# Four columns abreast in the head, pieces of 512, 384 and 128 features in the tail of a two-block network kernel

## The chip, the cores and the metric

The kernel runs on one core of a Trainium2 chip. Its metric is the device time of one execution in microseconds (us). A core has five engines that run side by side, each with its own order of instructions: TensorE (PE) multiplies matrices, VectorE (DVE) and ScalarE (ACT) work on elements, GpSimd (POOL) and SyncE (SP) do little here; SP issues most of the DMA transfers between the chip's memory (HBM) and the core's on-chip memory (SBUF). TensorE writes to PSUM, eight banks of 512 fp32 columns. Engines wait for each other by semaphores.

## The reference

256 tokens of 1024 features pass through two blocks. The first is a convolution branch and a latent attention branch, gated and added, with a convolutional feed-forward behind them; the second adds 16 meta tokens and runs stick-breaking attention, an MLP, a gated linear recurrence and another MLP. What the change touches is the very start and the very end:

```python
h = rms_norm(x, norm1_g[l])
proj = h @ w_in[l]
a_in, q_c, kv_c, k_rope_in, gates = split_cols(proj, IN_SPLITS)
val, gate = a[..., :CONV_WIDTH], a[..., CONV_WIDTH:]    # a is a_in
u = val * jax.nn.sigmoid(gate)
...
h = h + sq_relu_mlp(hn, mlp_w_up[i], mlp_w_down[i])
h = rms_norm_2(h, norm_final)
return h[:, N_META:]
```

`rms_norm` divides a token's features by the root of their mean square plus 1e-6 and multiplies by a gain.

## The kernel before

**Products.** Everything is fp32, and each product is made from three: a matrix w is split into `wh` (rounded to TensorE's short fp32 form) and `wl = w - wh`, the input x likewise into `Ah` and `Al` (`hh` and `hl` in an MLP), and wh·xh + wl·xh + wh·xl is summed in PSUM. All 128x128 weight blocks lie in HBM in the order of their use, 16 of them in a unit of 1 MB. The class `Stream` brings a unit into a buffer `raw` (three buffers), and splits each half unit (8 blocks): ScalarE casts `wh<-raw` (L229), VectorE subtracts `wl<-raw,wh` (L230). `split()` does the next half unit, `ahead()` runs it up to four halves before TensorE's position, `take()` hands out a block. TensorE runs through the blocks without gaps for nearly the whole kernel; the orders of TensorE and SP, and in the first section of all engines, are those of the code.

**Head.** x comes in four pieces of two 128-row chunks each (x has eight chunks k), between the four quarters of unit 0, all on SP's queue (L469, L222); unit 1 follows in two halves, then the vectors, unit 2 in one transfer, positions and constants. `first_part` (L238, L239) splits a quarter of unit 0, `x_split` makes `Ah` and `Al` of one chunk of x with the norm's gain. The norm's divisor is left out of the products: they are linear in x, and it is multiplied in behind them. For it ScalarE squares x (`sq`), VectorE adds the squares up to `sq0` (a tile named `acc` in the profile), and TensorE multiplies a matrix of ones with it, so that each column has its token's sum in all rows (`ps_tr<-acc,ones`); `rsqrt_row` makes `rstd` of that.

The first products are the convolution's four gates (columns 10 to 13) and four values (6 to 9). `linears` computes several output columns abreast: for each k one product for each column. `linear` computes one column over all k. Before, column 10 and 6 (channel 0) ran abreast, 16 blocks and so all of unit 0; then 11 and 7 one after the other (unit 1), then the ones-times-squares matmul, then columns 12, 8, 13, 9. `gate` multiplies by `rstd` and applies tanh, `glu` forms the gated value `upad`, and puts 31 convolution steps per channel on a list `bg`, from which `linear` takes `n_bg` at a time (`NB`).

**Tail.** The last matrix, `down1`, is used the other way round: `hh` and `hl` are the stationary side (128 tokens), the weights are moved through, so the output has tokens on partitions and 1024 features along the free axis. The tokens come in two halves a = 0, 1; `pieces` cuts the features of each half into PSUM tiles. The 32 inputs k run one after the other over all pieces (`down_product`, three matmuls each), but the last six (`TAIL`) are kept and run piece by piece, so that `finish` and `store` of a piece run beside the matmuls of the next. `finish(a, i)` adds the residual (VectorE, `xt<-ps_mm,r2t,xt`), squares with a sum per token (ScalarE, `sqt`, sum into column i of `sums`), and multiplies by the gain (`gx`). `store(a)` adds the columns of `sums`, takes the root (ScalarE, `rs`), the reciprocal (VectorE), scales the pieces (piece 1 on ScalarE, the others on VectorE) and stores them (piece 1 from ScalarE's queue, the others from SP's).

Of the kernel before, what the change touches and what calls it, by code (L numbers as in the profile page):

```python
# [36 lines left out]
NB = (3, 3, 2, 1, 5, 14)  # L37
# [78 lines left out]
# outputs that are summed side by side, one input chunk after the other  # L116
# [4 lines left out]
}  # L121


def weight_plan():
    plan = []

    def cols(name, c0, nk):
        for k in range(nk):
            plan.append((name, k, c0))

    def cols_abreast(name, c0s, nk):
        for k in range(nk):
            for c0 in c0s:
                plan.append((name, k, c0))

    def groups(name, nk):
        for ms in GROUPS[name]:
            for k in range(nk):
                for m in ms:
                    plan.append((name, k, m * P))  # L140

    cols_abreast("w_a", [10 * P, 6 * P], 8)
    for c in range(1, 4):
        cols("w_a", (6 + 4 + c) * P, 8)
        cols("w_a", (6 + c) * P, 8)
    for m in range(6):
        cols("w_a", m * P, 8)
    for m in range(8):
        cols("w_uq", m * P, 3)
    for m in range(4):  # L150
        cols("w_ukv", m * P, 2)
    for k in range(2):
        for m in range(4):
            plan.append(("w_ukv", k, 512 + m * P))
    for m in range(16):
        cols("w_g" if m in NAT_GATES else "w_a", (14 + m) * P, 8)
# [37 lines left out]
class Stream:  # L194
    """Weights in the order of their use: DMA, then the exact two-part split."""

    def __init__(self, nc, w_ap, raw_pool, split_pool):
        self.nc, self.w = nc, w_ap
        self.raw_pool, self.split_pool = raw_pool, split_pool
        self.raw, self.half, self.done = {}, {}, {}  # L200
        self.n_dma = self.n_half = self.pos = 0
        self.nhalf = (NBLK + HB - 1) // HB

    def dma(self):
        u = self.n_dma
        if u >= NU:
            return
        t = self.raw_pool.tile([P, UB * P], F32, tag="raw", name=f"raw{u}")
        n = min(UB, NBLK - u * UB) * P
        step = n // 2 if u == 1 else n  # L210
        for o in range(0, n, step):
            self.nc.sync.dma_start(out=t[:, o:o + step], in_=self.w[u][:, o:o + step])
        self.raw[u] = t
        self.done[u] = 0
        self.n_dma += 1

    def dma_first(self):
        t = self.raw[0] = self.raw_pool.tile([P, UB * P], F32, tag="raw", name="raw0")
        self.done[0] = 0
        self.n_dma = 1  # L220
        for o in range(0, UB * P, 512):
            self.nc.sync.dma_start(out=t[:, o:o + 512], in_=self.w[0][:, o:o + 512])  # L222
            yield
# [9 lines left out]
    def first_part(self, raw, i):  # L233
        """A quarter of the first unit, whose halves split() has only named."""
        hi, lo = self.half[i // 2]
        r = slice(i % 2 * 512, i % 2 * 512 + 512)
        src = raw[:, i * 512:(i + 1) * 512]
        self.nc.scalar.copy(out=hi[:, r], in_=src)  # L238
        self.nc.vector.tensor_tensor(out=lo[:, r], in0=src, in1=hi[:, r].bitcast(F32), op=ALU.subtract)  # L239
# [4 lines left out]
    def split(self):  # L244
# [10 lines left out]
        if self.native(h):  # L255
            self.half[h] = (src, None)
        else:
            hi = self.split_pool.tile([P, HB * P], F32R, tag="wh", name=f"wh{h}")
            lo = self.split_pool.tile([P, HB * P], F32R, tag="wl", name=f"wl{h}")
            self.half[h] = (hi, lo)  # L260
            if h > 1:
                self.parts(h, src, n, 512 if h < 4 else n)
            self.done[u] += 1
# [37 lines left out]
def build(tc, wall, x_t, meta_t, pos, vec, cst, gw, g_fin, out):  # L301
    nc = tc.nc
    ctx = ExitStack()
    with ctx:
# [14 lines left out]
        def mm_tile():  # L319
            return psum("mm", 3)  # L320
# [140 lines left out]
        # ------------------------------------------------------------ block 1  # L461
# [3 lines left out]
        with tc.manual_schedule(), tc.tile_pool(name="pro", bufs=1) as pro:  # L465
            nc.scalar.dma_start(out=vec_t[:, 0:8], in_=vec[:, 0:8])
            first = w.dma_first()
            for k, _ in zip(range(0, KD, 2), first):
                nc.sync.dma_start(out=xres[:, k:k + 2, R:], in_=x_t[:, k:k + 2, :])  # L469
            w.dma()  # L470
# [11 lines left out]
            tables("natural_log_exp_and_others")  # L482
# [5 lines left out]
            w.split()  # L488
            raw0 = w.raw[0]
            w.split()  # L490
            for i in range(4):
                w.first_part(raw0, i)
                x_split(2 * i)
                x_split(2 * i + 1)
# [36 lines left out]
        # rope factors  # L531
# [45 lines left out]
        for ch in range(4):  # L577
            pg, pv = mm_tile(), mm_tile()
            if ch == 0:
                linears("w_a", [10 * P, 6 * P], xa, 8, [pg[:, :S], pv[:, :S]])  # L580
            else:
                linear("w_a", (10 + ch) * P, xa, 8, pg[:, :S], n_bg=NB[0])
            tg = t272("ta", 3)

            def gate(tg=tg, pg=pg):
                paced(tt(tg[:, :S], pg[:, :S], rstd[:, :S]))
                act(out=tg[:, :S], in_=tg[:, :S], func=AF.Tanh, scale=0.5)

            if ch == 0:
                held = (tg, pv, gate)  # L590
                continue
            if ch > 1:
                gate()
            linear("w_a", (6 + ch) * P, xa, 8, pv[:, :S], n_bg=NB[0])
            if ch == 1:
# [4 lines left out]
                held[2]()  # L600
                glu(0, held[0], held[1])
                gate()
# [31 lines left out]
        # the norm of x * rstd: rstd / sqrt(mean(x^2) * rstd^2 + eps)  # L634
# [26 lines left out]
        # rotated key, shared by the heads  # L661
# [54 lines left out]
        def pv_mla(hp):  # L716
            """Two heads, side by side in the array."""
# [104 lines left out]
        # convolutional feed-forward  # L822
# [32 lines left out]
        # the first block's final norm and the second block's first one in one row  # L855
# [4 lines left out]
        # eps for the tokens that have no first norm  # L860
# [24 lines left out]
        def first_rows():  # L885
            # real tokens: r1 / sqrt(mean((x f)^2) r1^2 + eps) = 1 / sqrt(mean((x f)^2) + eps / r1^2)
# [12 lines left out]
        # ------------------------------------------------------------ stick-breaking attention  # L899
# [164 lines left out]
        # softplus(-lam) = max(-lam, 0) + 2 atanh(e / (2 + e)), e = exp(-|lam|)  # L1064
# [14 lines left out]
        # half of the log of a at r = 1  # L1079
# [24 lines left out]
        # ------------------------------------------------------------ RG-LRU  # L1104
# [30 lines left out]
        def gates(m):  # L1135
# [9 lines left out]
            # t = tanh(log(a) / 2): 1 - a^2 = -t (1 + a)^2  # L1145
# [60 lines left out]
        # the last projection, with the tokens on partitions  # L1206
# [23 lines left out]
        # the pieces of the features, for the two halves of the tokens  # L1230
        pieces = (((0, 512), (512, 512)), ((0, 512), (512, 256), (768, 256)))
# [10 lines left out]

        sums = tmp.tile([P, 2, 4], F32, tag="sums", name="sums", bufs=1)
# [11 lines left out]

        def store(a):
            s = tmp.tile([P, 1], F32, tag="nmx", name="total", bufs=2)
            nc.vector.tensor_reduce(out=s, in_=sums[:, a, :len(pieces[a])], axis=AX.X, op=ALU.add)
            act(out=rs[:, a:a + 1], in_=s, func=AF.Sqrt, scale=1.0 / D, bias=eps_t)
# [93 lines left out]
```

## Time and profile before

| | |
|---|---|
| times of three runs | 974.29, 974.38, 975.68 us; median 974.38 |
| span of the profiled execution | 972.0 us, 17931 instructions; its own device time is not given apart |
| TensorE's stage of the last projection | 873 to 965 us |
| last matmul starts | 964.76 us |
| first product matmul starts | 7.02 us |

The page has one execution. PE is TensorE's matmuls, PEld its weight loads, which run beside them; a "q" behind an engine's name is its queue of DMA issues. In a timeline a row has the start and the duration in us, the engine, the line of the kernel, the operation, out<-in, partitions x elements, and in brackets how long the engine stood idle before and which instruction released it. A matmul row's duration reaches over the start of the next, since matmuls are pipelined; what one costs in a dense stretch is the distance of the starts. An LDWEIGHTS row is the load of a matmul's stationary 128x128 matrix.

### The profile page before, as it was taken

Reading aid. Unit: us, or ns where it says so; the run is one execution under the profiler, and the core shown is the slowest. Engines: PE = TensorE matmul, PEld = TensorE weight load, DVE = VectorE, ACT = ScalarE, POOL = GpSimd, SP = SyncE. Lnnn points to the kernel's source line nnn. Section 1 sums busy time; section 2 is a strip of 40 time slices with the busy share of each in tenths; the row PEclk is TensorE's granted clock in tenths of the full one; section 3 lists DMA queues with packets and bytes.
Section 4 is the critical chain, followed back from the end, with each engine's and each line's share of the span. In section 5 each row is a group of like instructions: output and inputs, shape, how many; then the busy total and the mean of one; then the engine's idle time right before and its main releaser. Section 6 shows DMA issues by size and latency. Waiting matters only on the chain.

```text
span 972.0 us, 17931 instructions
## 1 busy us (share of the span) xinstructions
PE 962.1 (99%) x7350; PEld 923.9 (95%) x7350; DVE 688.5 (71%) x1215; ACT 597.3 (61%) x1037; POOL 6.7 (1%) x38
## 2 busy tenths in 40 slices
PE   9999999999999999999999999999999999999997
PEld 8988889999999999999999999999999999998886
DVE  6999888799999566876686555455587985554443
ACT  7855586777667546555556666444479687774332
POOL 0000000000000000000000000000000000000000
PEclk9999999999999999999999999999999999999999
DMA  8523365545554555333234554544452565555531
GB/s 310 196 86 131 130 223 187 199 172 181 197 190 174 180 182 203 107 111 130 88 131 174 174 177 174 180 173 174 174 208 88 210 222 197 175 178 177 201 117 43
DMA packets 26113, 163.39 MB, mean 168 GB/s; under 512 B 3888, under 2 KB 5424, under 8 KB 6960
## 3 DMA queue, kind: packets, MB, share of 16 engines
q1 hardware_dynamic: 25312, 160.29, 47.1%
q0 software_dynamic: 288, 1.57, 0.4%
q8 instruction: 57, 0.93, 0.4%
q10 hardware_dynamic: 432, 0.40, 0.1%
q14 instruction: 24, 0.20, 0.0%
HBM read 161.20 MB, written 1.05 MB: 167 GB/s over the span
## 4 chain that ended last, share of the span: by engine, by line
PE 95%; DVE 2%; ACT 1%; DMA 1%; issue 0%; SPq 0%; DVEq 0%; ACTq 0%
PE ps_mm L385 88%; PE ps_z L385 4%; PE ps_o L385 1%; PE ps_tr L385 1%; DVE wl L230 1%; DMA xres<-x_t 1%; DVE iu L1172 0%; ACT L346 0%; PE ps_tr L710 0%; DVE gt L379 0%; DVE iu L379 0%; DVE th L382 0%; PE ps_tr L973 0%; ACT th L350 0%; PE ps_tr L1227 0%
## 5 line engine op out<-in xcount | busy, mean ns | idle before, releaser
L230 DVE TENSOR_TENSOR wl<-raw,wh 128x1024 fp32r<-128x1024 f32 (+1 forms) x288 | 349.4, 1217 | 210.1 <-ACT wh L229 208.6
L229 ACT CAST wh<-raw 128x1024 fp32r<-128x1024 f32 (+1 forms) x288 | 298.5, 1042 | 222.1 <-PE ps_mm L385 217.7
L385 PE MATMUL ps_mm<-Ah,wh 128*128 128x256 f32 (+1 forms) x1360 | 390.2, 287 | 1.1 <-ACT Ah L350 1.1
L385 PE MATMUL ps_mm<-Ah,wl 128*128 128x256 f32 (+1 forms) x1360 | 386.5, 284 | 0.2 <-DVE wl L230 0.2
L385 PE MATMUL ps_mm<-Al,wh 128*128 128x256 f32 (+1 forms) x1360 | 385.3, 283 | 0.0
L385 PEld LDWEIGHTS ps_mm<-Ah,wh 128*128 128x128 f32 x1360 | 255.3, 188 | 2.1 <-ACT Ah L350 1.2
L385 PEld LDWEIGHTS ps_mm<-Al,wh 128*128 128x128 f32 x1360 | 256.6, 189 | 0.5 <-DVE Al L370 0.4
L385 PEld LDWEIGHTS ps_mm<-Ah,wl 128*128 128x128 f32 x1360 | 255.8, 188 | 1.0 <-DVE wl L230 0.6
L385 PE MATMUL ps_mm<-hl,wh 128*128 128x272 f32 (+1 forms) x432 | 123.5, 286 | 0.0
L385 PE MATMUL ps_mm<-hh,wh 128*128 128x272 f32 (+1 forms) x432 | 123.4, 286 | 0.0
L385 PE MATMUL ps_mm<-hh,wl 128*128 128x272 f32 (+1 forms) x432 | 123.3, 285 | 0.0
L385 PEld LDWEIGHTS ps_mm<-hh,wl 128*128 128x128 f32 x432 | 81.3, 188 | 0.0
L385 PEld LDWEIGHTS ps_mm<-hh,wh 128*128 128x128 f32 x432 | 81.3, 188 | 0.0
L385 PEld LDWEIGHTS ps_mm<-hl,wh 128*128 128x128 f32 x432 | 81.3, 188 | 0.0
L567 DVE SCALAR_TENSOR_TENSOR cacc<-upad,whalf,cacc 128x256 f32<-128x256 f32 x120 | 57.7, 482 | 1.6
L385 PE MATMUL ps_mm<-wh,hh 128*128 128x512 f32 (+1 forms) x160 | 56.0, 350 | 0.0
L385 PE MATMUL ps_mm<-wh,hl 128*128 128x512 f32 (+1 forms) x160 | 55.9, 349 | 0.0
L385 PE MATMUL ps_mm<-wl,hh 128*128 128x512 f32 (+1 forms) x160 | 55.8, 349 | 0.0
L350 ACT ACTIVATE ta<-ps_mm 128x272 f32<-128x272 f32 (+1 forms) x64 | 25.1, 392 | 49.1 <-PE ps_mm L385 49.0
L385 PE MATMUL ps_mm<-bl,wh 128*128 128x256 f32 (+1 forms) x160 | 45.7, 286 | 0.6 <-DVE bl L362 0.6
L385 PE MATMUL ps_mm<-bh,wh 128*128 128x256 f32 (+1 forms) x160 | 46.0, 288 | 0.0
L385 PE MATMUL ps_mm<-bh,wl 128*128 128x256 f32 (+1 forms) x160 | 45.5, 284 | 0.0
(246 smaller groups left out, 1230.9 us busy)
## 6 DMA issues: line engine op xcount, KB each, us to landing
raw<-wall SPq DMA_DIRECT2D x148, 1024.0 KB, 4.9
raw<-wall SPq DMA_DIRECT2D x3, 512.0 KB, 7.6
raw<-wall SPq DMA_DIRECT2D x4, 256.0 KB, 5.8
xres<-x_t SPq DMA_DIRECT2D x4, 256.0 KB, 6.0
gw_t<-gw POOLq DMA_DIRECT2D x1, 1024.0 KB, 7.9
g_t<-g_fin POOLq DMA_DIRECT2D x1, 512.0 KB, 3.4
out_t<-gx SPq DMA_DIRECT2D x2, 256.0 KB, 2.2
cst_t<-cst SPq DMA_DIRECT2D x1, 337.5 KB, 9.0
```

Of the source, the lines that this page charges most:

```text
L229: self.nc.scalar.copy(out=hi[:, r], in_=src[:, r])
L230: self.nc.vector.tensor_tensor(out=lo[:, r], in0=src[:, r], in1=hi[:, r].bitcast(F32), op=ALU.subtract)
L350: i = nc.scalar.activation(out=out, in_=in_, func=func, **kw)
L385: nc.tensor.matmul(out=out_, lhsT=lhsT, rhs=rhs, start=start, stop=stop, skip_group_check=True)
L567: paced(nc.vector.scalar_tensor_tensor(out=cacc[:, ch, :], in0=upad[:, ch, j:j + S], scalar=wj, in1=cacc[:, ch, :], op0=ALU.mult, op1=ALU. ...
```

## The change

At the head, four columns abreast (10, 6, 11, 7, two channels) for each k take the place of two abreast and two in a row, so units 0 and 1 are used together with x, a quarter unit (four blocks) for each chunk k. x comes in eight pieces of one chunk: four on ScalarE's queue (with the load of ScalarE's function tables moved behind them), four on SP's between the quarters of unit 1, which now comes in four transfers like unit 0. Unit 2, one transfer of 1 MB as before, is the one that is cast in 512-column steps between the squares. The ones-times-squares matmul stands after the gate column of channel 2 (120 product matmuls ahead of it, not 96), and the gates of channels 0 and 1 behind it. `NB[1]` is 4.

At the tail, token half 1 is cut into 512, 384 and 128 features. `finish` forms a running `part` (sum of squares / 1024 plus eps, or plus the part before) on VectorE for all pieces but the last, and `store` takes the root of the last piece's sum with `part` as its bias, without the reduction `total`.

```diff
-NB = (3, 3, 2, 1, 5, 14)
+NB = (3, 4, 2, 1, 5, 14)
...
+FIRST = [10 * P, 6 * P, 11 * P, 7 * P]
...
-    cols_abreast("w_a", [10 * P, 6 * P], 8)
-    for c in range(1, 4):
+    cols_abreast("w_a", FIRST, 8)
+    for c in range(2, 4):
...
             nc.scalar.dma_start(out=vec_t[:, 0:8], in_=vec[:, 0:8])
-            first = w.dma_first()
-            for k, _ in zip(range(0, KD, 2), first):
-                nc.sync.dma_start(out=xres[:, k:k + 2, R:], in_=x_t[:, k:k + 2, :])
-            w.dma()
+            for k in range(4):
+                nc.scalar.dma_start(out=xres[:, k, R:], in_=x_t[:, k, :])
+            tables("natural_log_exp_and_others")
+            for _ in w.dma_parts():
+                pass
+            second = w.dma_parts()
+            for k, _ in zip(range(4, KD), second):
+                nc.sync.dma_start(out=xres[:, k, R:], in_=x_t[:, k, :])
+            next(second, None)
...
-            for i in range(4):
-                w.first_part(raw0, i)
-                x_split(2 * i)
-                x_split(2 * i + 1)
+            for _ in range(4):
+                w.split()
+            for i in range(KD):
+                w.first_part(i)
+                x_split(i)
...
+        heads = [mm_tile() for _ in FIRST]
+        linears("w_a", FIRST, xa, 8, [p_[:, :S] for p_ in heads])
+        for ch in range(2, 4):
             pg, pv = mm_tile(), mm_tile()
...
-            if ch == 1:
+            linear("w_a", (10 + ch) * P, xa, 8, pg[:, :S], n_bg=NB[0])
+            if ch == 2:
                 t = psum("tr", 2)
                 mm(t[:, :S], ones, sq0, True, True)
                 rsqrt_row(t[:, :S], rstd[:, :S], D)
                 tables("exp_and_others")
-                held[2]()
-                glu(0, held[0], held[1])
-                gate()
+                for c_ in range(2):
+                    glu(c_, gate(heads[2 * c_]), heads[2 * c_ + 1])
+            tg = gate(pg)
+            linear("w_a", (6 + ch) * P, xa, 8, pv[:, :S], n_bg=NB[0])
...
-        pieces = (((0, 512), (512, 512)), ((0, 512), (512, 256), (768, 256)))
+        pieces = (((0, 512), (512, 512)), ((0, 512), (512, 384), (896, 128)))
...
+            if i < len(pieces[a]) - 1:
+                s = tmp.tile([P, 1], F32, tag="sm%d" % (i % 2), name="part", bufs=2)
+                stt(s, sums[:, a, i:i + 1], 1.0 / D, part.get(a, eps_t), ALU.mult, ALU.add)
+                part[a] = s
...
-            s = tmp.tile([P, 1], F32, tag="nmx", name="total", bufs=2)
-            nc.vector.tensor_reduce(out=s, in_=sums[:, a, :len(pieces[a])], axis=AX.X, op=ALU.add)
-            act(out=rs[:, a:a + 1], in_=s, func=AF.Sqrt, scale=1.0 / D, bias=eps_t)
+            act(out=rs[:, a:a + 1], in_=sums[:, a, n - 1:n], func=AF.Sqrt, scale=1.0 / D, bias=part[a])
```

ScalarE in the head, behind the last quarter of unit 0. Before: the quarter's cast and the last two chunks of x, then unit 1 (`raw_105`) in steps of 512 columns with the squares between, then unit 2 (`raw_109`). "Waits DMAHW..." is a wait for a transfer.

```order
L238 CAST wh_137<-raw_96 128x512 [waits DMAHW7_49]
L350 ACTIVATE Ah<-xres,vec_t 128x256 [waits DMAHW0_49]
L350 ACTIVATE Ah<-xres,vec_t 128x256
L229 CAST wh_165<-raw_105 128x512 [waits DMAHW1_49]
L229 CAST wh_165<-raw_105 128x512
L350 ACTIVATE sq_131<-xres 128x512
L350 ACTIVATE sq_132<-xres 128x512
L229 CAST wh_174<-raw_105 128x512 [waits DMAHW2_49]
L229 CAST wh_174<-raw_105 128x512
L350 ACTIVATE sq_133<-xres 128x512
L350 ACTIVATE sq_134<-xres 128x512
```

Of the change, from the last quarter of unit 1 (`raw_106`) on; `raw_116` is unit 2.

```order
L243 CAST wh_149<-raw_106 128x512 [waits DMAHW7_49]
L357 ACTIVATE Ah<-xres,vec_t 128x256 [waits DMAHW0_49]
L357 ACTIVATE nones_r<-ones 128x128 [waits DVE_49]
L357 ACTIVATE l_6262<-vec_t 128x8 [waits DMAHW1_49]
L234 CAST wh_185<-raw_116 128x512 [waits DMAHW2_49]
L234 CAST wh_185<-raw_116 128x512
L357 ACTIVATE sq_137<-xres 128x512
L357 ACTIVATE sq_138<-xres 128x512
L234 CAST wh_194<-raw_116 128x512 x2
L357 ACTIVATE sq_139<-xres 128x512
L357 ACTIVATE sq_140<-xres 128x512
```

The squares stood behind the first half of unit 1, and stand now behind the first half of unit 2, whose arrival all four wait for in ScalarE's order.

TensorE in the last projection, one input k: the last three of its five tiles before, the pieces of token half 1 (`ps_mm_10638` is its first piece, 10639 and 10640 the others).

```order
L385 MATMUL ps_mm_10638<-wh293_11059,hh_9451 128x512
L385 MATMUL ps_mm_10638<-wl293_11060,hh_9451 128x512
L385 MATMUL ps_mm_10638<-wh293_11059,hl_9452 128x512
L385 MATMUL ps_mm_10639<-wh293_11059,hh_9451 128x256
L385 MATMUL ps_mm_10639<-wl293_11060,hh_9451 128x256
L385 MATMUL ps_mm_10639<-wh293_11059,hl_9452 128x256
L385 MATMUL ps_mm_10640<-wh293_11059,hh_9451 128x256
L385 MATMUL ps_mm_10640<-wl293_11060,hh_9451 128x256
L385 MATMUL ps_mm_10640<-wh293_11059,hl_9452 128x256
```

The same of the change.

```order
L392 MATMUL ps_mm_10648<-wh293_11069,hh_9461 128x512
L392 MATMUL ps_mm_10648<-wl293_11070,hh_9461 128x512
L392 MATMUL ps_mm_10648<-wh293_11069,hl_9462 128x512
L392 MATMUL ps_mm_10649<-wh293_11069,hh_9461 128x384
L392 MATMUL ps_mm_10649<-wl293_11070,hh_9461 128x384
L392 MATMUL ps_mm_10649<-wh293_11069,hl_9462 128x384
L392 MATMUL ps_mm_10650<-wh293_11069,hh_9461 128x128
L392 MATMUL ps_mm_10650<-wl293_11070,hh_9461 128x128
L392 MATMUL ps_mm_10650<-wh293_11069,hl_9462 128x128
```

The matmuls stay in number and order; three of them per k are wider by 128 columns and three narrower.

VectorE at the very end, from the second piece of token half 1 on, before.

```order
L382 SCALAR_TENSOR_TENSOR xt<-ps_mm,r2t,xt 128x256 [waits PE_49]
L379 TENSOR_TENSOR gx<-xt,g_t 128x256 [waits DVE_49]
L382 SCALAR_TENSOR_TENSOR xt<-ps_mm,r2t,xt 128x256 [waits PE_49]
L379 TENSOR_TENSOR gx<-xt,g_t 128x256 [waits DVE_49]
L1258 TENSOR_REDUCE total<-sums 128x1 [waits Activation_49]
L1260 RECIPROCAL rs_10642<-rs_10642 128x1 [waits Activation_49]
```

And of the change, from the same piece's place on.

```order
L389 SCALAR_TENSOR_TENSOR part<-sums,eps_t 128x1 [waits Activation_49]
L389 SCALAR_TENSOR_TENSOR xt<-ps_mm,r2t,xt 128x384 [waits PE_49]
L386 TENSOR_TENSOR gx<-xt,g_t 128x384 [waits DVE_49]
L389 SCALAR_TENSOR_TENSOR part<-sums,part 128x1 [waits Activation_49]
L389 SCALAR_TENSOR_TENSOR xt<-ps_mm,r2t,xt 128x128 [waits PE_49]
L386 TENSOR_TENSOR gx<-xt,g_t 128x128 [waits DVE_49]
L1268 RECIPROCAL rs_10652<-rs_10652 128x1 [waits Activation_49]
```

The reduction behind the last piece is gone; a sum of one column stands ahead of the second and of the third piece, and waits for ScalarE's squares of the piece before.

More of the change, by code (lines that the diff above doesn't have):

```diff
@@ L200, in __init__ @@
         self.raw, self.half, self.done = {}, {}, {}
+        self.first = {}
         self.n_dma = self.n_half = self.pos = 0
@@ L209, in dma @@
         n = min(UB, NBLK - u * UB) * P
-        step = n // 2 if u == 1 else n
-        for o in range(0, n, step):
-            self.nc.sync.dma_start(out=t[:, o:o + step], in_=self.w[u][:, o:o + step])
+        self.nc.sync.dma_start(out=t[:, :n], in_=self.w[u][:, :n])
         self.raw[u] = t
@@ L215, in dma, with dma_parts @@
         self.n_dma += 1
[L217 to L220, printed above, removed]
+    def dma_parts(self):
+        u = self.n_dma
+        t = self.raw[u] = self.raw_pool.tile([P, UB * P], F32, tag="raw", name=f"raw{u}")
+        self.done[u] = 0
+        self.n_dma += 1
         for o in range(0, UB * P, 512):
-            self.nc.sync.dma_start(out=t[:, o:o + 512], in_=self.w[0][:, o:o + 512])
+            self.nc.sync.dma_start(out=t[:, o:o + 512], in_=self.w[u][:, o:o + 512])
             yield
@@ L231, in parts, with first_part @@
                                          op=ALU.subtract)
-    def first_part(self, raw, i):
+    def first_part(self, i):
         hi, lo = self.half[i // 2]
         r = slice(i % 2 * 512, i % 2 * 512 + 512)
-        src = raw[:, i * 512:(i + 1) * 512]
+        src = self.first[i // 4][:, i % 4 * 512:(i % 4 + 1) * 512]
         self.nc.scalar.copy(out=hi[:, r], in_=src)
@@ L260, in split @@
             self.half[h] = (hi, lo)
-            if h > 1:
-                self.parts(h, src, n, 512 if h < 4 else n)
+            if h > 3:
+                self.parts(h, src, n, 512 if h < 6 else n)
+            else:
+                self.first[u] = self.raw[u]
             self.done[u] += 1
@@ L481, in build @@
                 mm(warm[:, :P], ones, ones, True, True)
-            tables("natural_log_exp_and_others")
             sq = [pro.tile([P, 2, S], F32, tag="sq%d" % k, name="sq%d" % k) for k in range(4)]
@@ L486, in x_split @@
                 split_g(xres[:, k, R:], v("norm1_g", k), ah[:, k, :S], al[:, k, :S])
-            w.split()
-            raw0 = w.raw[0]
-            w.split()
-            for i in range(4):
-                w.first_part(raw0, i)
-                x_split(2 * i)
-                x_split(2 * i + 1)
+            for _ in range(4):
[3 more added lines that the diff above has]
+                x_split(i)
             w.split()
@@ L575, in glu, with gate @@
                 bg.append(lambda ch=ch, j=j: conv_tap(ch, j))
-        for ch in range(4):
-            pg, pv = mm_tile(), mm_tile()
[L579 to L592, printed above, removed]
-                gate()
-            linear("w_a", (6 + ch) * P, xa, 8, pv[:, :S], n_bg=NB[0])
-            if ch == 1:
+        def gate(pg):
+            tg = t272("ta", 3)
+            paced(tt(tg[:, :S], pg[:, :S], rstd[:, :S]))
+            act(out=tg[:, :S], in_=tg[:, :S], func=AF.Tanh, scale=0.5)
+            return tg
+        heads = [mm_tile() for _ in FIRST]
+        linears("w_a", FIRST, xa, 8, [p_[:, :S] for p_ in heads])
+        for ch in range(2, 4):
+            pg, pv = mm_tile(), mm_tile()
+            linear("w_a", (10 + ch) * P, xa, 8, pg[:, :S], n_bg=NB[0])
+            if ch == 2:
                 t = psum("tr", 2)
@@ L599, in build @@
                 tables("exp_and_others")
-                held[2]()
-                glu(0, held[0], held[1])
-                gate()
+                for c_ in range(2):
+                    glu(c_, gate(heads[2 * c_]), heads[2 * c_ + 1])
+            tg = gate(pg)
+            linear("w_a", (6 + ch) * P, xa, 8, pv[:, :S], n_bg=NB[0])
             glu(ch, tg, pv)
@@ L1241, in down_product @@
             mm(o, hl[:, k, ra], wh[:, rc], False, k == NH2 - 1)
+        part = {}
         sums = tmp.tile([P, 2, 4], F32, tag="sums", name="sums", bufs=1)
@@ L1254, in finish @@
             tt(gx[:, a, c0:c0 + n], xm, g_t[:, c0:c0 + n])
+            if i < len(pieces[a]) - 1:
+                s = tmp.tile([P, 1], F32, tag="sm%d" % (i % 2), name="part", bufs=2)
+                stt(s, sums[:, a, i:i + 1], 1.0 / D, part.get(a, eps_t), ALU.mult, ALU.add)
+                part[a] = s
         def store(a):
-            s = tmp.tile([P, 1], F32, tag="nmx", name="total", bufs=2)
-            nc.vector.tensor_reduce(out=s, in_=sums[:, a, :len(pieces[a])], axis=AX.X, op=ALU.add)
-            act(out=rs[:, a:a + 1], in_=s, func=AF.Sqrt, scale=1.0 / D, bias=eps_t)
+            n = len(pieces[a])
+            act(out=rs[:, a:a + 1], in_=sums[:, a, n - 1:n], func=AF.Sqrt, scale=1.0 / D, bias=part[a])
             nc.vector.reciprocal(out=rs[:, a:a + 1], in_=rs[:, a:a + 1])
```

## The prediction

> **What bounds the kernel now.** I read the page from the top: the span, the engines' shares, then the chain that ended last.
>
> ```profile
> span 972.0 us, 17931 instructions
> PE 962.1 (99%) x7350; PEld 923.9 (95%) x7350; DVE 688.5 (71%) x1215; ACT 597.3 (61%) x1037; POOL 6.7 (1%) x38
> ...
> PEclk9999999999999999999999999999999999999999
> ...
> PE 95%; DVE 2%; ACT 1%; DMA 1%; issue 0%; SPq 0%; DVEq 0%; ACTq 0%
> ```
>
> TensorE works for 99% of the span at a full clock, and 95% of the chain is its matmuls. So a change pays only if it shortens TensorE's own stream, or the two ends where TensorE does not run: the start-up and the 7 us behind the last matmul. There are 7350 weight loads (PEld) for 7350 matmuls: every matmul brings its own load. The next view, busy time by stage, has us, then busy us and instructions of PE, PEld, DVE, ACT and POOL, granted clock, DMA share, GB/s.
>
> ```profile
> 7.00:14.00 7.00, 6.95 (x49) 6.19 (x49) 6.00 (x13) 6.05 (x13) 0.00 (x0) 1.00 1.04 399
> 14.00:20.00 6.00, 6.00 (x50) 5.89 (x50) 5.63 (x12) 5.49 (x10) 1.13 (x1) 1.00 1.02 406
> ...
> 41.00:130.00 89.00, 89.00 (x535) 78.38 (x534) 82.41 (x194) 52.25 (x119) 0.00 (x0) 1.00 0.38 131
> ...
> 900.00:950.00 50.00, 50.00 (x269) 42.80 (x268) 21.58 (x19) 18.89 (x18) 0.00 (x0) 1.00 0.42 149
> 950.00:972.00 22.00, 15.03 (x83) 12.82 (x81) 8.59 (x18) 5.03 (x14) 0.00 (x0) 0.90 0.13 48
> ```
>
> Two things matter here. In the last projection (900 to 950 us) TensorE has no gap at all while VectorE and ScalarE stand idle more than half the time: what a matmul costs there is time of the kernel, one for one. In the head (7 to 20 us) the DMA engines are full at about 400 GB/s, so data that is needed early comes no sooner than the bytes ahead of it allow.
>
> **The tail's matmuls (the largest term).** For each of 32 inputs k, token half 1 had nine products 512, 256, 256 columns wide (three each), and gets 512, 384, 128. The number of matmuls and of columns stays. This is TensorE's timeline in that stage; a start minus the one before is what a matmul costs, since neighbours overlap.
>
> ```profile
> 944.54 0.28 PE L385 MATMUL ps_mm<-wh,hh 128*128 128x256 f32 x1
> ...
> 945.25 0.40 PE L385 MATMUL ps_mm<-wh,hh 128*128 128x512 f32 x1
> ...
> 947.35 0.28 PE L385 MATMUL ps_mm<-wh,hh 128*128 128x256 f32 x1
> ```
>
> Six 256-wide ones take 945.25 - 944.54 = 0.71 us, 0.118 each; nine 512-wide ones 947.35 - 945.25 = 2.10, 0.233 each. A straight line between them gives 0.176 for 384 columns and 0.061 for 128, and with these 3 x (0.176 + 0.061) = 0.71: no change. But that line holds only while the columns are what takes the time. The trace has narrower matmuls, and they don't follow it (PE and PEld, each in its timeline; x4 and x16 are rows run together):
>
> ```profile
> 790.19 0.50 PE L385 MATMUL ps_tr<-ones,acc 128*128 128x1 f32 x4
> 790.55 0.36 PE L385 MATMUL ps_mm<-Ah,wh 128*128 128x256 f32 x1
> ...
> 790.07 0.54 PEld L385 LDWEIGHTS ps_tr<-ones,acc 128*128 128x128 f32 x4
> 790.52 0.19 PEld L385 LDWEIGHTS ps_mm<-Ah,wh 128*128 128x128 f32 x1
> ...
> 873.28 1.77 PEld L1227 LDWEIGHTS ps_tr<-cst_t,xres 128*128 128x128 f32 x16
> 875.02 0.19 PEld L385 LDWEIGHTS ps_mm<-wh,hh 128*128 128x128 f32 x1
> ...
> 395.03 0.46 PE L385 MATMUL ps_z<-sh,ntri_r 128*128 128x432 f32 x1
> 395.33 0.23 PE L385 MATMUL ps_z<-sh,nones_r 128*128 128x144 f32 x1
> 395.40 0.41 PE L385 MATMUL ps_z<-sl,ntri_r 128*128 128x432 f32 x1
> 395.64 0.23 PE L385 MATMUL ps_z<-sl,nones_r 128*128 128x144 f32 x1
> ```
>
> Four matmuls that move one single column have weight loads that start (790.52 - 790.07) / 4 = 0.1125 us apart, and sixteen 128x128 transposes (875.02 - 873.28) / 16 = 0.109. One column or 128, it is the same: a full 128x128 load takes about 0.11 us, and the next can be prepared only while one matmul runs. Against this speaks a start only 0.07 us after a 144-wide matmul (395.33 to 395.40); but the 432-wide one that follows takes 0.24 us to the next start (395.40 to 395.64), where the line gives 0.20, so the pair costs 0.31, which is 0.20 for the columns and 0.11 for a load, not 0.27. The load is paid there too.
>
> So I take 0.1115 us (between 0.109 and 0.1125, nearest to the transposes and to the single columns alike) for a 128-wide matmul, and 0.176 for a 384-wide one, whose load hides. A k costs 3 x (0.176 + 0.1115) - 0.71 = +0.152 us, and 32 of them **+4.85 us**. Bounds: with 0.109 it is 96 x (0.109 - 0.061) = +4.6; if a narrow load in this type cost as much as a whole 256-wide matmul, 0.118, it would be +5.5; if loads can be prepared further ahead, so that the 384-wide ones' slack covers them (6 x 0.111 = 0.67 is below 0.71), it is 0. The last is a rival below.
>
> The Trainium skill, page "TensorE: Matmul & The Clock Gate", section "Back-to-back issue gap", gives about 81 ns per matmul for a sustained stream of loads and 128-column matmuls, and about 56 ns for an isolated one; by the first this term would be 96 x (0.081 - 0.061) = +1.9 us, by the second nothing. The rows above, 0.109 and 0.1125, speak against both.
>
> **The tail's end.** Behind the last matmul:
>
> ```profile
> 964.76 0.28 PE L385 MATMUL ps_mm<-wh,hl 128*128 128x256 f32 x1
> ...
> 965.07 0.48 DVE L382 SCALAR_TENSOR_TENSOR xt<-ps_mm,r2t,xt 128x256 f32<-128x256 f32 x1 [1.19 <-PE ps_mm L385]
> ...
> 966.19 0.16 DVE L1258 TENSOR_REDUCE total<-sums 128x1 f32<-128x3 f32 x1 [0.18 <-ACT sqt L350]
> ...
> 965.65 0.42 ACT L350 ACTIVATE sqt<-xt 128x256 f32<-128x256 f32 x1 [1.68 <-DVE xt L382]
> 965.98 0.19 ACT L350 ACTIVATION_READ_ACCUMULATOR sqt<-xt 128x1 f32 x1
> 966.38 0.29 ACT L350 ACTIVATE rs<-total,eps_t 128x1 f32<-128x1 f32 x1 [0.22 <-DVE total L1258]
> ...
> L382 DVE SCALAR_TENSOR_TENSOR xt<-ps_mm,r2t,xt 128x512 f32<-128x512 f32 x3 | 2.3, 752 | 6.0 <-PE ps_mm L385 6.0
> L350 ACT ACTIVATE sqt<-xt 128x512 f32<-128x512 f32 x3 | 1.9, 637 | 9.4 <-DVE xt L382 9.4
> ```
>
> The chain is last matmul, residual on VectorE, square on ScalarE, sum, root, reciprocal, scale, store; 972.0 - 964.76 = 7.24 us. At 128 columns the residual is shorter by half the step from 256 to 512, (0.752 - 0.48) / 2 = 0.14; the square likewise by (0.637 - 0.42) / 2 = 0.11; the matmul's own end by some 0.05 (a 144-wide one lasts 0.23, not 0.28). The sum of the three parts goes, with its hand-over: 966.38 - 966.19 = 0.19, of which the direct wait of the root on the square's sums keeps a little; I take -0.17. Together **-0.45** (between -0.2, if only the reduction goes, and -0.7, if the hand-overs halve). The added 128x1 sums stand on VectorE between a piece and the next and wait for ScalarE; behind them waits the next residual, which waits for TensorE anyway (1.19 us in the row above). The 384 piece has 18 x 0.1115 = 2.0 us of the last piece's matmuls for its residual, square and sum, by the rows about 0.62 + 0.53 (half way between 256 and 512 again) + 0.19 (the sums read out) + 0.16 plus hand-overs, some 1.7: covered, by 0.3 us; uncovered, a sum would cost its 0.16. The 384-wide scaling on ScalarE takes about 0.1 longer than the 256 one, beside the 512-wide on VectorE, whose store is issued last.
>
> **The head.** Four columns abreast ask for x half as fast, so TensorE's small stalls there should go.
>
> ```profile
> 6.46 0.91 ACT L350 ACTIVATE Ah<-xres,vec_t 128x256 fp32r<-128x256 f32 x2 [1.48 <-DMA xres<-x_t]
> 12.68 1.15 ACT L229 CAST wh<-raw 128x512 fp32r<-128x512 f32 x2 [0.37 <-DMA raw<-wall]
> 17.10 2.01 ACT L229 CAST wh<-raw 128x1024 fp32r<-128x1024 f32 x2
> ...
> 18.24 0.43 DVE L379 TENSOR_TENSOR acc<-sq 128x256 f32<-128x256 f32 x1
> ...
> 7.02 0.39 PE L385 MATMUL ps_mm<-Ah,wh 128*128 128x256 f32 x1 [1.05 <-ACT Ah L350]
> ...
> 19.76 0.59 PE L385 MATMUL ps_tr<-acc,ones 128*128 128x256 f32 x2
> ...
> 26.32 0.39 PE L385 MATMUL ps_mm<-Ah,wl 128*128 128x256 f32 x1 [0.16 <-DVE wl L230]
> ...
> raw<-wall SPq DMA_DIRECT2D x1, 1024.0 KB, 9.1
> ```
>
> From 7.02 to 26.32 stand 145 product matmuls (145 x 0.118 = 17.1) and the ones-times-squares pair (19.76; 0.47 in steps), so 1.7 us are stalls: that is all the head can gain while the first matmul waits for x at 6.46. What takes their place is the squares. They stood between the casts of unit 1, whose first half came at 12.68, and `acc` was ready at 18.24 + 0.43 = 18.67, 6.0 us later. Now all of unit 1 is cast with x, and the squares stand behind and between the casts of unit 2, which is one transfer of 1 MB. It was issued 9.1 us before it landed, just ahead of the casts at 17.10. The bytes ahead of it are the same (x and units 0 and 1 at 1 MB each, 0.2 MB of vectors), over full DMA engines, so it lands at about 17.2 again. The same four half-unit casts and squares follow: `acc` at 17.2 + 6.0 = 23.2. TensorE, without stalls, has done its 120 products at 7.02 + 120 x 0.118 = 21.2 and waits **2.0 us** there, with every later product behind it. Then 0.47 and 25 products: 23.2 + 0.47 + 25 x 0.118 = 26.6 for the matmul that was at 26.32, **+0.3**. Bounds: unit 2 earlier by 2 us or more, -1.7; later by 1 us, +1.3.
>
> Downstream, the root row and the two gated products come some 5 us later, and the 62 convolution steps behind them. From 41 to 130 us VectorE was busy 82.4 of 89 us: 6.6 us of room, just enough. If not, lost time there is below 1 us; I put none. The fourth background step per chunk (3 to 4) only spreads them.
>
> **Sum.** 972.0 + 4.85 - 0.45 + 0.3 = 976.7 for the span. The median of the runs shown is 974.38, 2.4 above the profiled span; the page gives no device time for the profiled execution, so I take those 2.4 us to lie around the span: **979.1 us**.
>
> **Rivals.**
> 1. *Loads run ahead* (the other side). If several loads can be prepared while a 384 or 512 runs, the 128s stream at 0.061, the first term is 0 and the time 974.3, not slower; it decides from the point where a 128-wide spacing falls below 0.075. For it: the one start 0.07 apart. Against it: the pair's 0.31, and sixteen transposes that never got below 0.109. If the head gains too, 972.3. Chance 0.08, a third of it faster.
> 2. *81 ns a matmul*, loads partly hidden: 979.1 - 4.85 + 1.9 = 976.1. Chance 0.05. This is the rate of the Trainium skill's section named above.
> 3. *The head gains*: unit 2, or x, lands early enough that TensorE finds `acc` ready: 979.1 - 0.3 - 1.7 = 977.1. For it: the first halves and x come in smaller pieces over two queues; against: the DMA engines were already full. Chance 0.15.
> 4. *The head loses*: more transfers with a fixed number in flight, so unit 2 is issued and lands 1.5 us late, and the wait at the squares grows: 980.6. Chance 0.13.
>
> My forecast has 0.59. The range 976.6 to 981.2 takes in rivals 3 and 4 and the bounds of the first term, and leaves out rivals 1 and 2 and the far ends. A measurement of this kernel tells about 0.2% (1.95 us) from no change: slower than 976.33 is 0.86, within 0.09, faster 0.05.
>
> **What would show it.** In the last projection 128-wide matmuls start 0.11 us apart (0.06: rival 1; 0.08: rival 2), and a k takes 2.96 us instead of 2.81. Behind the last matmul 6.8 us instead of 7.24, with the root straight behind the square. The ones-times-squares matmul waits about 2 us for `acc`, near 23 us; no wait there is rival 3. The first matmul near 7.0. The forecast is wrong at once if the last projection is not some 4.9 us longer.

## The result: 0.69% slower, by two terms that add up

The changed kernel takes 980.89 us (median of 4 runs, 980.65 to 981.87) against 974.34 us before; the ratio is 1.0069, 95% interval 1.0056 to 1.0082. The profiled execution spans 979.1 us, 7.0 more than before (979.05 and 972.04 by the traces; the page rounds). The chain and the stages of the changed kernel's page, in the columns used before:

```profile
span 979.1 us, 17945 instructions
...
PE 88%; DVE 7%; DMA 2%; ACT 1%; issue 1%; SPq 0%; ACTq 0%; DVEq 0%
...
7.00:14.00 7.00, 6.12 (x49) 5.91 (x50) 5.90 (x12) 6.11 (x13) 0.00 (x0) 1.00 0.88 283
...
900.00:950.00 50.00, 50.00 (x255) 43.12 (x254) 20.83 (x17) 17.48 (x18) 0.00 (x0) 1.00 0.45 158
```

In the last projection TensorE is still busy in all of the 50 us, but gets through 255 matmuls, not 269. Its share of the chain fell by 7 points, from 95% to 88%; VectorE got five of them, the transfers and the issuing one each. For the first 66 us the chain now runs almost wholly through transfers, the casts and squares on ScalarE and VectorE's splits and convolution steps. TensorE's timeline at four places, the head, the convolution's norm, the start and the end of the last projection:

```profile
7.87 0.39 PE L392 MATMUL ps_mm<-Ah,wh 128*128 128x256 f32 x1 [1.35 <-ACT Ah L357]
...
24.14 0.70 PE L392 MATMUL ps_tr<-acc,ones 128*128 128x256 f32 x2 [1.53 <-DVE acc L386]
...
138.00 1.35 PE L392 MATMUL ps_tr<-upad,ones 128*128 128x256 f32 x5 [0.79 <-ACT upad L357]
...
878.21 0.47 PE L392 MATMUL ps_mm<-wh,hh 128*128 128x512 f32 x1
...
972.53 0.27 PE L392 MATMUL ps_mm<-wh,hl 128*128 128x128 f32 x1
```

Setting matmul n of one kernel beside matmul n of the other (both have 7350) gives how late the changed kernel is:

| place | before, us | after, us | late by |
|---|---|---|---|
| first product matmul | 7.02 | 7.87 | 0.85 |
| 146th product matmul (end of the head) | 26.32 | 27.63 | 1.31 |
| first block products of the attention branch's queries | 63.78 | 65.67 | 1.88 |
| ones times `upad` (convolution's norm) | 135.07 | 138.00 | 2.94 |
| first matmul of the last projection | 875.05 | 878.21 | 3.16 |
| last matmul | 964.76 | 972.53 | 7.77 |
| end | 972.04 | 979.05 | 7.01 |

So 3.2 us are lost ahead of the last projection, nearly all of it in the first 140 us, 4.6 in the last projection, and 0.76 are won behind the last matmul. Single profiles scatter: in the six that have the code of before up to the last projection, it starts between 874.96 and 876.04 us, so a few tenths ahead of it mean nothing. Inside the last projection the kernels that share its code agree to 0.01 us.

### The profile page after: what moved, and what is told of

Its sections match the earlier page's. It is cut to its first block, busy times and chain, and to the rows that moved or that the text cites. A ratio compares the mean times of both kernels' runs of the same rounds, so it can differ in the third digit from the quotient of the medians.

```text
span 979.1 us, 17945 instructions
## 1 busy us (share of the span) xinstructions
PE 967.2 (99%) x7350; PEld 928.5 (95%) x7350; DVE 689.1 (70%) x1218; ACT 596.1 (61%) x1039; POOL 6.7 (1%) x38
## 4 chain that ended last, share of the span: by engine, by line
PE 88%; DVE 7%; DMA 2%; ACT 1%; issue 1%; SPq 0%; ACTq 0%; DVEq 0%
PE ps_mm L392 82%; PE ps_z L392 4%; DVE wl L235 2%; DVE cacc L576 2%; DMA raw<-wall 1%; PE ps_o L392 1%; DMA xres<-x_t 1%; PE ps_tr L392 1%; DVE iu L1175 0%; DVE gt L386 0%; DVE iu L386 0%; DVE th L389 0%; PE ps_tr L976 0%; ACT L353 0%; ACT th L357 0%
## 5 line engine op out<-in xcount | busy, mean ns | idle before, releaser
L392 PE MATMUL ps_mm<-wh,hh 128*128 128x512 f32 (+2 forms) x160 | 57.9, 362 | 0.0
L392 PE MATMUL ps_mm<-wh,hl 128*128 128x512 f32 (+2 forms) x160 | 57.4, 358 | 0.0
L392 PE MATMUL ps_mm<-wl,hh 128*128 128x512 f32 (+2 forms) x160 | 57.2, 357 | 0.0
```

What stands on the lines that cost most here:

```text
L392: nc.tensor.matmul(out=out_, lhsT=lhsT, rhs=rhs, start=start, stop=stop, skip_group_check=True)
```

## The experiments

Eleven kernels ran; each time stands beside runs of the kernel before on the same chip.

### The tail

**Part and bias alone.** The kernel before with `part` and the root's bias, pieces still 512, 256, 256.

```diff
+                stt(s, sums[:, a, i:i + 1], 1.0 / D, part.get(a, eps_t), ALU.mult, ALU.add)
...
-            nc.vector.tensor_reduce(out=s, in_=sums[:, a, :len(pieces[a])], axis=AX.X, op=ALU.add)
-            act(out=rs[:, a:a + 1], in_=s, func=AF.Sqrt, scale=1.0 / D, bias=eps_t)
+            act(out=rs[:, a:a + 1], in_=sums[:, a, n - 1:n], func=AF.Sqrt, scale=1.0 / D, bias=part[a])
```

> The kernel before with the running part and the root's bias alone, pieces 512, 256, 256. My theory, that the sum behind the last square is what this edit removes: the way from the last matmul to the end falls from 7.24 to about 7.0 us, all else stays, about 974.1 us (-0.2). Rival, that the added sums hold VectorE up ahead of the last piece: no gain, or 974.5. Theory and rival lie within the noise of the time; the distance from the last matmul to the end tells them apart.

Measured: 973.55 us, ratio 0.9992 (0.9983 to 1.0001). From the last matmul to the end it is 7.08 us by the trace instead of 7.29, and 7.10 in the kernel with `NB[1]` at 4 below, which has the same tail: the 0.2 of the theory. But "all else stays" was wrong. From the first to the last matmul of the last projection it takes 88.82 us (874.96 to 963.78), where the kernel before has 89.71; the two other kernels below with part, bias and pieces of 256 have 88.82 too, and the head alone, with the old tail, 89.71. The 512-wide matmuls start closer there, nine of them in 2.04 us, before in 2.09 (the kernel before, then this one):

```profile
951.55 0.40 PE L385 MATMUL ps_mm<-wh,hh 128*128 128x512 f32 x1
...
953.64 0.39 PE L385 MATMUL ps_mm<-wh,hh 128*128 128x512 f32 x1
```

```profile
951.43 0.39 PE L385 MATMUL ps_mm<-wh,hh 128*128 128x512 f32 x1
...
953.47 0.39 PE L385 MATMUL ps_mm<-wh,hh 128*128 128x512 f32 x1
```

Why an edit of VectorE's and ScalarE's work does that is not shown.

**The whole tail on the old head.**

```diff
-        pieces = (((0, 512), (512, 512)), ((0, 512), (512, 256), (768, 256)))
+        pieces = (((0, 512), (512, 512)), ((0, 512), (512, 384), (896, 128)))
```

(with part and bias as above)

> The head of before with the whole tail of the change (pieces 512, 384, 128, part and bias). Theory, that a 128-wide matmul costs a weight load, 0.11 us: +4.8 in the last projection, -0.65 behind the last matmul, together +4.1, 978.4 us. Rival, that the growth between 875 us and the last matmul comes from the later start of the stream (another phase of the transfers, or splits that fall behind): at most +0.5, 974.8 or less.

Measured: 978.76 us, ratio 1.0045 (1.0031 to 1.0059), +4.6 beside 974.13. The stretch of one input k in its timeline:

```profile
940.34 0.34 PE L385 MATMUL ps_mm<-wh,hh 128*128 128x384 f32 x1
940.52 0.34 PE L385 MATMUL ps_mm<-wl,hh 128*128 128x384 f32 x1
940.69 0.34 PE L385 MATMUL ps_mm<-wh,hl 128*128 128x384 f32 x1
940.87 0.23 PE L385 MATMUL ps_mm<-wh,hh 128*128 128x128 f32 x1
940.93 0.28 PE L385 MATMUL ps_mm<-wl,hh 128*128 128x128 f32 x1
941.04 0.27 PE L385 MATMUL ps_mm<-wh,hl 128*128 128x128 f32 x1
941.15 0.45 PE L385 MATMUL ps_mm<-wh,hh 128*128 128x512 f32 x1
941.45 0.40 PE L385 MATMUL ps_mm<-wl,hh 128*128 128x512 f32 x1
```

The 384-wide ones start 0.175 apart, as the line through 256 and 512 has it. Behind the first narrow one the next starts after 0.06, then 0.11 and 0.11, and the 512-wide one behind them lasts 0.45 and takes 0.30 to the next start instead of 0.235. The row whose start is early contains the wait, so the distances are read as a sum: 0.06 + 0.11 + 0.11 + 0.30 = 0.58 against 3 x 0.061 + 0.235 = 0.42 for columns alone, 0.16 too much for three narrow matmuls. From one input to the next it takes 2.96 us, before 2.81.

**Other widths.** 448 and 64, then 320 and 192, on the old head with part and bias.

```diff
-        pieces = (((0, 512), (512, 512)), ((0, 512), (512, 256), (768, 256)))
+        pieces = (((0, 512), (512, 512)), ((0, 512), (512, 448), (960, 64)))
```

> Head of before, part and bias, pieces 512, 448, 64. If the narrow matmul costs the load of its 128x128 stationary matrix whatever its width, a 64-wide one takes 0.11 us as well, the 448-wide one 0.204: 3 x (0.204 + 0.1115) - 0.71 = 0.237 us for each k, +7.6 for 32, less some 0.75 behind the last matmul: 981.1 us. Rival, a slow rate per column of narrow matmuls (0.11 for 128 columns, so 0.056 for 64): +2.2 less 0.75, 975.8 us. If columns alone count: 973.6.

Measured: 980.91 us, ratio 1.0071 (1.0058 to 1.0083), +6.8. With 64 columns the starts are the same 0.11 apart:

```profile
941.94 0.19 PE L385 MATMUL ps_mm<-wh,hh 128*128 128x64 f32 x1
941.97 0.27 PE L385 MATMUL ps_mm<-wl,hh 128*128 128x64 f32 x1
942.08 0.28 PE L385 MATMUL ps_mm<-wh,hl 128*128 128x64 f32 x1
942.19 0.48 PE L385 MATMUL ps_mm<-wh,hh 128*128 128x512 f32 x1
942.50 0.40 PE L385 MATMUL ps_mm<-wl,hh 128*128 128x512 f32 x1
```

A price per column is excluded (it gave +1.5), and so is a stream without loads. The load is a floor.

```diff
+        pieces = (((0, 512), (512, 512)), ((0, 512), (512, 320), (832, 192)))
```

> Head of before, part and bias, pieces 512, 320, 192. A 192-wide matmul has columns for 0.090 us and a load of 0.11, a 320-wide one takes 0.147: 3 x (0.147 + 0.1115) - 0.71 = 0.066 us for each k, +2.1 for 32, less some 0.35 behind the last matmul, 976.0 us. Rival, that loads hide from a smaller width than 256 on (192 columns cover them): 973.9.

Measured: 976.07 us, ratio 1.0014 (1.0005 to 1.0023), +1.3 beside 974.73, where the floor gives 2.1 - 0.35 = 1.75 and the rival a small gain. The timeline, too, has it on the side of the floor: the narrow ones' starts at 941.68, .77, .88 and the 512-wide ones' at .99 and 942.25 make 0.57, where columns alone give 3 x 0.089 + 0.235 = 0.50.

A least price of 0.11 us for any pair of load and matmul, whatever the load's size, would fit all these widths as well. Against it speak smaller loads in the kernel before:

```profile
401.36 0.19 PEld L385 LDWEIGHTS ps_o<-wt,vv 16*64 16x64 f32 x4 [0.20 <-issue]
401.58 0.19 PEld L385 LDWEIGHTS ps_mm<-Ah,wh 128*128 128x128 f32 x1
```

Four loads of 64 columns have passed 0.22 us after the first began, when the next product's load starts; at 0.11 a pair they would take 0.44. So the price goes with the load. These loads also fill 16 rows instead of 128, and the two are not told apart here.

**Wide and narrow in turns.** In the first 26 inputs each 384-wide matmul is followed by the 128-wide one with the same stationary matrix.

```diff
-            for a in range(2):
-                for i in range(len(pieces[a])):
-                    down_product(k, ws, a, i)
...
+            wh, wl = ws
+            for j, (x, y) in enumerate(((hh, wh), (hh, wl), (hl, wh))):
+                for i in (1, 2):
+                    c0, n = pieces[1][i]
+                    mm(outs[1][i][:, :n], x[:, k, P:2 * P], y[:, c0:c0 + n], k == 0 and j == 0, False)
```

> The tail of the change on the head of before, but in the first 26 inputs k each 384-wide matmul is followed by the 128-wide one with the same stationary matrix, so that no two narrow ones stand in a row. Theory, that one load is prepared beside one matmul: a 128-wide matmul still covers only 0.06 us of the 0.11 us load behind it, the cost stays, 978.8 us as in the tail alone. Rival, that several loads are prepared ahead and only a row of three narrow ones empties that stock: with wide ones between them the loads hide (0.176 + 0.061 is more than two loads), 26/32 of the cost goes, about 974.8 us.

Measured: 978.01 us, ratio 1.0038 (1.0024 to 1.0052), +3.6 beside 974.45. In the timeline a row x2 is a 384-wide matmul and the 128-wide one behind it:

```profile
942.14 0.39 PE L385 MATMUL ps_mm<-wh,hh 128*128 128x384 f32 x2
942.38 0.45 PE L385 MATMUL ps_mm<-wl,hh 128*128 128x384 f32 x2
942.66 0.45 PE L385 MATMUL ps_mm<-wh,hl 128*128 128x384 f32 x2
942.95 0.45 PE L385 MATMUL ps_mm<-wh,hh 128*128 128x512 f32 x1
943.23 0.39 PE L385 MATMUL ps_mm<-wl,hh 128*128 128x512 f32 x1
```

From 942.14 to 943.23 it is 1.09 us, with the narrow ones in a row 1.11 (940.34 to 941.45), by columns alone 0.95. Most of the cost stays: an input takes 2.93 us, with the narrow ones in a row 2.96, before 2.81. A wide neighbour hides little of the load behind a narrow one; what the 0.03 are was not tried.

### The head

**The head alone** (the change's head, the old tail).

> The change's head with the tail of before. Theory, that head and tail add up: 980.9 - 4.1 = 976.8, +2.5, with the first product matmul at 7.8 instead of 7.0, a wait of 1.5 us ahead of the ones-times-squares matmul and a further us at the convolution's norm near 138 us. Rival, that the delay up to 140 us is taken up again later in the kernel, where the transfers or the splits had been late anyway: 974.3 to 974.8.

Measured: 976.56 us, ratio 1.0023 (1.0013 to 1.0033), +2.4. Head and tail add up: 2.4 + 4.6 = 7.0 by the medians, against 6.6 for both.

**The squares ahead of unit 2's casts.**

```diff
-            w.split()
-            for k in range(2):
+            for k in range(4):
                 act(out=sq[k], in_=xres[:, 2 * k:2 * k + 2, R:], func=AF.Square)
-            tt(sq[0], sq[0], sq[1], ALU.add)
-            w.split()
-            for k in range(2, 4):
-                act(out=sq[k], in_=xres[:, 2 * k:2 * k + 2, R:], func=AF.Square)
-            for k in range(2, 4):
+            for k in range(1, 4):
                 tt(sq[0], sq[0], sq[k], ALU.add)
...
+            w.split()
+            w.split()
```

> The change's head (tail of before) with the squares of x and their sum moved ahead of the casts of unit 2 on ScalarE and VectorE. Theory, that the ones-times-squares matmul waits because the squares wait for unit 2: acc is ready near 19 us, the wait of 1.5 us is gone, 975.0 us against 976.6. Rival, that unit 2's splits then come late and stop TensorE at its first block instead (needed near 19.5 us): at least half of the 1.5 us comes back there, 976 or more.

Measured: 975.31 us, ratio 1.0008 (0.9999 to 1.0017). ScalarE and VectorE, and TensorE's ones-times-squares matmul, of the head alone and then of this kernel:

```profile
17.72 1.14 ACT L234 CAST wh<-raw 128x512 fp32r<-128x512 f32 x2 [2.16 <-DMA raw<-wall]
18.76 1.15 ACT L357 ACTIVATE sq<-xres 128x512 f32<-128x512 f32 x2
...
23.27 0.42 DVE L386 TENSOR_TENSOR acc<-sq 128x256 f32<-128x256 f32 x1
...
23.75 0.70 PE L392 MATMUL ps_tr<-acc,ones 128*128 128x256 f32 x2 [1.64 <-DVE acc L386]
```

```profile
15.11 2.18 ACT L357 ACTIVATE sq<-xres 128x512 f32<-128x512 f32 x4
...
18.60 0.42 DVE L386 TENSOR_TENSOR acc<-sq 128x256 f32<-128x256 f32 x1
...
22.52 0.59 PE L392 MATMUL ps_tr<-acc,ones 128*128 128x256 f32 x2
```

ScalarE had stood idle for 2.16 us ahead of unit 2 with the squares queued behind it. Put in front, they fill that gap, `acc` is there 4.7 us sooner, and the wait of 1.64 us is gone; 0.35 of it comes back at the first block of unit 2. The wait was the order's.

**x on one queue.**

```diff
-            for k in range(4):
-                nc.scalar.dma_start(out=xres[:, k, R:], in_=x_t[:, k, :])
             tables("natural_log_exp_and_others")
-            for _ in w.dma_parts():
-                pass
-            second = w.dma_parts()
-            for k, _ in zip(range(4, KD), second):
-                nc.sync.dma_start(out=xres[:, k, R:], in_=x_t[:, k, :])
-            next(second, None)
+            for u in range(2):
+                for k, _ in zip(range(4 * u, 4 * u + 5), w.dma_parts()):
+                    nc.sync.dma_start(out=xres[:, k, R:], in_=x_t[:, k, :])
```

> The change's head (tail of before) with all eight pieces of x on SyncE's queue, each behind a quarter of unit 0 or 1, and the table load where it was before. Theory, that the first pieces on ScalarE's queue share the transfers' engines with three quarters of unit 0, land late (the fifth piece was issued only at 7.2 us, when the first had landed) and so delay everything behind them, unit 2 too: first matmul near 6.3 instead of 7.8, unit 2's casts near 17.2 instead of 18.1, 975.5 to 975.9 us. Rival, that the number of transfers in flight is what limits, on whichever queue: unit 2 as late as in the change, 976.6.

Measured: 976.5 us, ratio 1.0019 (1.001 to 1.0028): nothing against the head alone. My theory fell by half. The first matmul did come 1.4 us sooner (5.87 against 7.29), but unit 2's casts start at 17.77 (17.72 in the head alone) and the ones-times-squares matmul at 23.80 (23.75). What TensorE wins at the start it loses at the wait.

**NB[1] back at 3**, on the change's head.

> The change's head (tail of before) with NB[1] back at 3. Theory, that the step of 1 us near 138 us (VectorE has two splits ahead of the centring of the convolution) comes from the later place of the convolution's steps, not from this number: with 3 the steps end later still, 976.6 to 978. Rival, that the four steps per chunk are what disturbs the order there: 975.6.

Measured: 980.2 us, ratio 1.0065 (1.0051 to 1.0079), +5.7 beside 974.45, where the head alone, with 4, has +2.4: slower by some 3.3 us, beyond either value. TensorE at the sums for the convolution's norm, and VectorE's last step ahead of it:

```profile
136.22 0.70 PE L392 MATMUL ps_tr<-cacc,ones 128*128 128x256 f32 x2 [3.28 <-DVE cacc L576]
...
135.68 0.48 DVE L576 SCALAR_TENSOR_TENSOR cacc<-upad,whalf,cacc 128x256 f32<-128x256 f32 x1
```

The convolution's first step on VectorE is at 38.7 here (31.6 before), and with three steps per chunk the last one ends at 136.2, when TensorE has already stood there for 3.28 us. With four they end by 128.6 in the changed kernel.

**NB[1] at 4 on the old head** (with part and bias).

```diff
-NB = (3, 3, 2, 1, 5, 14)
+NB = (3, 4, 2, 1, 5, 14)
```

> The kernel before with the part and bias (512, 256, 256) and NB[1] at 4, its head as it was. Theory, that four steps per chunk put both splits ahead of the centring of the convolution in VectorE's order, and that this alone costs the step near 138 us: the ones-times-upad matmuls move back by about 1 us against the same kernel with 3, 974.5 us against 973.6. Rival, that the step needs the late convolution of the new head: no step, 973.6.

Measured: 974.16 us, ratio 0.9994 (0.9985 to 1.0003); the time alone doesn't tell it from part and bias alone (0.9992). The traces do: matmul by matmul this kernel is 0.43 us later than part and bias alone from 26 us up to the convolution's norm, and 1.10 from there on, a step of 0.67 instead of the 1 us expected. VectorE, with 3 steps and then with 4:

```profile
130.95 1.22 DVE L230 TENSOR_TENSOR wl<-raw,wh 128x1024 fp32r<-128x1024 f32 x1
132.25 1.23 DVE L379 TENSOR_TENSOR cacc<-cacc,mu 128x1024 f32<-128x1024 f32 x1
```

```profile
131.29 2.36 DVE L230 TENSOR_TENSOR wl<-raw,wh 128x1024 fp32r<-128x1024 f32 x2 [0.41 <-ACT wh L229]
133.57 1.22 DVE L379 TENSOR_TENSOR cacc<-cacc,mu 128x1024 f32<-128x1024 f32 x1
```

With four, a second split stands ahead of the centring, which TensorE's next matmul waits for through ScalarE's square. So the step near 138 us belongs to the number 4 and does not need the late convolution; 0.67 us stand here, 0.95 in the changed kernel.

**Squares first, x on one queue, part and bias, pieces of 256**: the attempt at a better kernel.

> The change's head with x on one queue and the squares ahead of unit 2's casts, part and bias, pieces 512, 256, 256. Theory, that with the squares out of the way TensorE can use the earlier start and waits only for unit 2 itself (casts near 17.8, first block wanted at 17.2): about 1 us better than with the squares moved alone, and 0.3 from the bias, 974.0 us, no better than before because the step near 138 us stays. Rival, that unit 3 or the convolution then bound the head, so that the earlier start is lost again: 975.0.

Measured: 973.87 us, ratio 0.9992 (0.9983 to 1.0001). No better than part and bias alone, nor to be told from the kernel before. The earlier start is again lost, this time at unit 2 itself: TensorE stands 1.07 us at 19.82 for its first cast. In this profile unit 2's casts start at 19.14, 1.4 us later than with x on one queue alone, which the theory had not expected and no run explains.

## Why the prediction was right, and where a term was too small

The forecast was +4.7 (979.1), and +6.5 came; 980.89 lies in the range of 976.6 to 981.2. The largest term, the loads, was right in mechanism and size. That the sum still came within the range is in part luck: VectorE's 1.8 us further down had no place in it, and the range reached up to 981.2 for rival 4 (980.6) and the loads' upper bound. The span came 2.3 us above its forecast of 976.7; the 2.4 us taken to lie around it were 1.9 in the profiled execution (981.01), which hides half a microsecond.

- *128-wide matmuls cost a load, +4.85.* Right. An input takes 2.96 us instead of 2.81, the two numbers forecast. The last projection grew by 7.77 - 3.16 = 4.61 and not by 4.85 because in the last six inputs 512-wide matmuls start closer, nine in 2.04 us, as with part and bias alone. Beside that kernel, whose last projection is 0.89 us shorter than before, the widths cost 5.5 us by the traces and 978.76 - 973.55 = 5.2 by the times. The runs with 64 and 192 columns and the one with wide and narrow in turns exclude a rate per column and loads prepared further ahead (rival 1), and narrow matmuls 0.11 apart exclude 0.081 (rival 2). The Trainium skill's page "TensorE: Matmul & The Clock Gate", section "Back-to-back issue gap", gives about 81 ns for a sustained stream of loads and 128-column matmuls; the traces here do not agree, with 0.11 us.
- *Behind the last matmul, -0.45.* 6.53 us instead of 7.29, -0.76, beyond the bound of -0.7. The tail's own part is the -0.45 forecast: 6.84 against 7.29 for the tail alone on the old head, 6.53 against 6.98 for the change beside the head alone. From the residual's start to the root's it is 973.72 - 972.84 = 0.88, where it was 966.38 - 965.07 = 1.31: -0.43, the savings of residual, square and sum; the matmul's own end gave nothing (0.31 both times). The other -0.31 comes with the head, which has 6.98 with the old tail too; it lies behind the issue of the last store, and its cause is open.

```profile
972.18 0.16 DVE L389 SCALAR_TENSOR_TENSOR part<-sums,part 128x1 f32<-128x1 f32 x1
972.84 0.35 DVE L389 SCALAR_TENSOR_TENSOR xt<-ps_mm,r2t,xt 128x128 f32<-128x128 f32 x1 [0.50 <-PE ps_mm L392]
...
973.72 0.29 ACT L357 ACTIVATE rs<-sums,part 128x1 f32<-128x1 f32 x1
```

The added sum was covered by 0.50 us, as VectorE's idle time shows.

- *The squares wait for unit 2; TensorE waits for the squares.* The mechanism is right and shown by moving them: a wait of 1.53 us at 24.14 (2.0 at 23.2 forecast). The term of +0.3 was mis-sized: +1.31. It took unit 2 to land as before, at 17.2, and the casts start at 18.09; in the head alone, with x on either queue, at 17.7 to 17.8. That is rival 4's way, by less than its 1.5 us: SyncE issued unit 2 three microseconds later (before, then after).

```profile
7.98 0.33 SPq L212 DMA_DIRECT2D raw<-wall  x1
```

```profile
10.93 0.43 SPq L215 DMA_DIRECT2D raw<-wall  x1
```

Ahead of it SyncE's queue stood 2.2 and 2.1 us for earlier transfers to land. The sum counted the same bytes over full engines, but from 7 to 14 us they moved 283 GB/s, where the kernel before had 399, at a busy share of 0.88 instead of 1.04. Whether the waits or the smaller pieces cause that was not tried by itself. The size of this term is rough: the 146th product matmul is at 26.14 to 27.20 us in the seven profiles with the old head, and at 27.25 to 27.83 in three with the new one (the change, the head alone, `NB[1]` at 3).

- *Downstream: nothing; NB[1] only spreads.* This step failed, by about 1.8 us (3.16 - 1.31). The room of 6.6 us on VectorE was too small: with three steps per chunk the late convolution stops TensorE for 3.28 us. Four steps cure that at the price of a split ahead of the centring, 0.95 us near 138 us. Another 0.6 are lost near 64 us, where two of TensorE's loads come late because VectorE's step `qp`, which reads an earlier product out of PSUM, is late; one of them:

```profile
65.67 0.51 PEld L392 LDWEIGHTS ps_mm<-qc,raw 128*128 128x128 f32 x3 [0.52 <-DVE qp L389]
```

This step stands in the head alone as well, and neither in the new head with three steps nor in the old head with four (one profile each), so it seems to need both. The remaining 0.3 is drift, within the noise of one profile.

## What to carry to other kernels

A matmul that moves fewer columns than its weight load takes time for is paid at the load's price: cutting a last piece in half to shorten the way to the end is worth it only if it happens a few times, not in all 32 inputs (0.45 us won, the shorter sum included, and 4.6 paid). When loads are moved about at the start, follow what stands behind them in each engine's order: here four squares that needed nothing but x stood behind a 1 MB transfer. And a start that is 1.4 us sooner is worth nothing if the next unit's arrival sets the pace.

## What was not expected of the hardware

A load's floor shows in the row behind it: a narrow matmul's successor starts 0.03 to 0.06 us later by the trace and then lasts longer (0.27 to 0.28 us for 64 and 128 columns alike, against 0.19 and 0.23 for the first of the three), so one pair of starts, like the 0.07 that spoke for rival 1, understates the cost, and only the sum up to a later start has it. And a 512-wide matmul does not cost the same in every kernel: 0.227 to 0.233 us in rows of nine, with nothing changed in TensorE's own order.
